# Chunked-scan stage of an encoder layer: decay prepared two chunks earlier and masked one chunk earlier, a second buffer for transposed outputs, the last group's steps over three gate blocks

## Chip, cores and metric

The kernel runs on one core of one Trainium2 chip. The metric is the device time of one launch in microseconds (us). Three runs of the kernel before took 2399.12, 2401.84 and 2405.68 us; the median is 2401.84 us. The profile is one more execution of the same program.

## What is computed

One encoder layer on 1024 tokens of width 1024, in fp32. Two token mixers read the same normed input: windowed attention with a learned sink (16 query heads, 4 key heads), and a Mamba-2 scan in both directions (32 heads in 8 groups, chunks of 128 tokens, state 128). Their outputs are projected, weighted by sigmoid gates and merged; then follow a cross-attention to 256 memory rows, a squared-ReLU MLP and a last norm. The change lies in the scan, cut here to what matters:

```
    CB = jnp.einsum('bclgn,bcsgn->bcgls', Cc, Bc)
    Wd = CB[:, :, :, None] * segsum_exp(adt)
    y_diag = jnp.einsum('bcgrls,bcsgrp->bclgrp', Wd, xdt)
    ...
    y_off = jnp.einsum('bclgn,bcgrpn,bcgrl->bclgrp', Cc, prev, jnp.exp(a_cs))
    return (y_diag + y_off).reshape(b, l, H, P)
```

`segsum_exp` is a 128x128 triangle of decays, one per head and chunk, with one triangle for each direction. `CB` is the same for the four heads of a group. After the scan, y is multiplied by silu(z) and normed within its group.

## The kernel before, in words

Every weight product on TensorE (PE) is done as three fp32r matmuls, high times high, high times low and low times high (`mm3`, the lines L85, L89 and L90); a weight tile comes by DMA and is split by ScalarE (ACT, `whi`, L66) and GpSimd (POOL, `wlo`, L69). One such product of a 128-wide weight block with all tokens has 48 matmuls, and the generator `fm_chunks` gives control back after every three, so a block has 16 units.

The scan stage (`ssd_phase`) is a list of such blocks, the jobs. For each group g there are four convolution blocks (x in two halves, then B, then C; `conv_job`), one gate block (`gate_job`) and the z block of 64 smaller units (`z_job`). While the weight products of group g run, the eight scan steps of group g-1 (chunks 7 down to 0) are slipped in: the dictionary beside each job says after which unit which piece is issued, so steps stand eight units apart. PE's order in this stage is this written order. The other engines' orders are set by a scheduler that may lift an instruction ahead of others where its inputs and buffers allow.

A step is `step(q, c)`, lines 519 to 553. It first calls `prep(q, c - 1)` for the next chunk: two DMAs from ACT's queue bring the rows of cumulated decay (`rows`, L503), POOL masks each triangle (L504, L506), ACT takes eight exponentials (`ef`, `eb`, L514 and L515), VectorE (DVE) adds the two directions (L516), PE makes `cb` = C·B (L509) and DVE multiplies `ef` by it (L517). `ef` has two buffers. Then the step itself: four matmuls of the masked decay with x (L529, into the free half of `cb`), one with the carried states (`yo`, L533), DVE scales that by the decay (`t`, L537, one buffer), POOL adds the skip term to the backward half (`p1`, L541 and L543), DVE adds the parts and multiplies by silu(z) (`yz`, L545 to L547), and ACT squares for the norm (L548). After four steps `rstd_of` (L122 on DVE, L124 on POOL) gives the norm, ACT scales the four `yz` tiles (L552), and `yt` transposes them on PE (L560); ACT copies the result to `yts` (L562, one buffer), which a DMA of SyncE's queue writes out. `cb`, `yo`, `yt`, `tm`, `st` and `zp` share one pool of PSUM slots: `yo` of a step goes into the slot that `t` of the step before has read, and the second half of `tm_b` (the transposed B, L456) into the slot of the first `yt`.

The last group has no following group to hide in. Its eight steps stand in gate blocks 8 and 9, four units apart. Gate blocks 10 to 14 belong to the attention stage that follows (`ATT_GATES`, L30), where a scheduler sets PE's order too: 10 beside key head 0, 11 beside 1, 12 beside 2, 13 and 14 beside 3.

Of the kernel before, what the change touches and what calls it, by code (L numbers as in the profile page):

```python
# [7 lines left out]
F32 = mybir.dt.float32  # L8
# [8 lines left out]
P = 128  # L17
# [9 lines left out]
SLOPES = [2.0 ** (-0.5 * (h + 1)) for h in range(16)]  # L27


ATT_GATES = ((10,), (11,), (12,), (13, 14))  # L30
END_GATE = 15


# [40 lines left out]
def wload(kx, src, n=1024, hi=None, lo=None, eng=None, pin=False):  # L74
    if hi is None:
        hi = kx.wp.tile([P, 1024], F32R, tag="wop", bufs=6, name="whi")[:, :n]
        lo = kx.wp.tile([P, 1024], F32R, tag="wop", bufs=6, name="wlo")[:, :n]
    split_in(kx, src, hi, lo, eng, pin)
    return hi, lo
# [39 lines left out]
def rstd_of(kx, pool, ss, n, width, eps):  # L119
    nc = kx.nc  # L120
    v = pool.tile([P, 8], F32, tag="rv", bufs=4, name="rv")
    nc.vector.tensor_scalar(v[:, :n], ss, 1.0 / width, eps, ALU.mult, ALU.add)  # L122
    r = pool.tile([P, 8], F32, tag="rr", bufs=4, name="rr")
    nc.gpsimd.tensor_tensor(r[:, :n], v[:, :n], kx.mhalf[:, :n], ALU.pow)  # L124
    return r
# [203 lines left out]

class Group:  # L330
    def __init__(self, g):
        self.g, self.hs, self.cx = g, slice(4 * g, 4 * g + 4), []


def fm_chunks(kx, ps, w, halves=(0, 1)):
    ws = wsplit(w)
    for h in halves:
        for k in range(NK):
            mm3(kx, ps[:, h * 512:(h + 1) * 512], ws[k], act_pair(kx.hT[h], k), k == 0, k == NK - 1)
            yield  # L340


def psum_g(kx, name):
    return kx.pg.tile([P, S], F32, tag="g", name=name)
# [46 lines left out]
def ssd_phase(kx, ins, dr):  # L391
# [3 lines left out]
    V, A, G, PE = nc.vector, nc.scalar, nc.gpsimd, nc.tensor  # L395
    with tc.tile_pool(name="p1", bufs=1) as sp, tc.manual_schedule(engines={mybir.EngineType.PE}):
# [4 lines left out]
        def heads(ap):  # L401
            return ap.rearrange("p (h q) -> p h q", h=4)
# [13 lines left out]
        def gate_job(m):  # L416
            def load():
                return wload(kx, ins["wg"][m])

            def run(w):  # L420
                ps = psum_g(kx, "gps")
                yield from fm_chunks(kx, ps, w)
                gt = ca.tile([P, 2, 512], F32, tag="tab", bufs=2, name="gt")
                for h in range(2):
                    A.activation(gt[:, h], ps[:, h * 512:(h + 1) * 512], AF.Tanh, scale=0.5)
                    nc.sync.dma_start(dr.gt[m][h], gt[:, h])
            return load, run
# [68 lines left out]

        def prep(q, c):
            b, j = c // 4, c % 4
            cl = slice(c * P, (c + 1) * P)
            rows = sp.tile([P, 2, 4, P], F32, tag="rows", bufs=2, name="rows")  # L500
            for d in range(2):
                o = 64 * d + 32 * b + 4 * q.g
                nc.scalar.dma_start(rows[:, d], dr.cs[o:o + 4, j * P:(j + 1) * P].partition_broadcast(P))  # L503
            G.affine_select(out=rows[:, 0], in_=rows[:, 0], compare_op=ALU.is_ge, fill=NEG, base=0,  # L504
                            pattern=[[0, 4], [1, P]], channel_multiplier=-1)
            G.affine_select(out=rows[:, 1], in_=rows[:, 1], compare_op=ALU.is_ge, fill=NEG, base=0,  # L506
                            pattern=[[0, 4], [-1, P]], channel_multiplier=1)
            q.cb = cb = kx.pp.tile([P, 512], F32, tag="p", name="cb")
            PE.matmul(cb[:, :P], q.BT[:, cl], q.CT[:, cl], start=True, stop=True)  # L509
            q.ef = ef = sp.tile([P, 4, P], F32, tag="ef", bufs=2, name="ef")  # L510
            eb = sp.tile([P, 4, P], F32, tag="eb", bufs=2, name="eb")
            for h in range(4):
                o = 4 * q.g + h
                A.activation(ef[:, h], rows[:, 0, h], AF.Exp, bias=kx.ebias[:, b, j, 0, o:o + 1])  # L514
                A.activation(eb[:, h], rows[:, 1, h], AF.Exp, bias=kx.ebias[:, b, j, 1, o:o + 1])  # L515
            V.tensor_tensor(ef, ef, eb, ALU.add)  # L516
            V.tensor_tensor(ef, ef, cb[:, :P].unsqueeze(1).broadcast_to([P, 4, P]), ALU.mult)  # L517

        def step(q, c):

            b, j = c // 4, c % 4
            cl = slice(c * P, (c + 1) * P)
            cb, ef = q.cb, q.ef
            if c:
                prep(q, c - 1)
            if j == 3:
                q.yz, q.ss = [None] * 4, sp.tile([P, 4], F32, tag="ss", bufs=2, name="ss")
            for h in range(4):
                PE.matmul(cb[:, 256 + 64 * h:256 + 64 * h + 64], ef[:, h], q.xtok[:, c, 64 * h:64 * h + 64],  # L529
                          start=True, stop=True)  # L530
            lo, hi = (256 if c == 0 else 0), (256 if c == NT - 1 else 512)
            yo = kx.pp.tile([P, 512], F32, tag="p", name="yo")
            PE.matmul(yo[:, lo:hi], q.CT[:, cl], q.prev[:, c].rearrange("p d q -> p (d q)")[:, lo:hi],  # L533
                      start=True, stop=True)
            d0, d1 = lo // 256, hi // 256
            t = sp.tile([P, 2, 256], F32, tag="t", bufs=1, name="t")
            V.tensor_tensor(t[:, d0:d1].rearrange("p d (h q) -> p d h q", h=4),  # L537
                            yo[:, lo:hi].rearrange("p (d h q) -> p d h q", h=4, q=64),
                            kx.ecs[:, b, j, d0:d1, q.hs].unsqueeze(3).broadcast_to([P, d1 - d0, 4, 64]), ALU.mult)
            p1 = sp.tile([P, 256], F32, tag="p1", bufs=2, name="p1")  # L540
            G.tensor_tensor(heads(p1), heads(q.xtok[:, c]), dsk[:, q.hs].unsqueeze(2).broadcast_to([P, 4, 64]), ALU.mult)  # L541
            if d1 - d0 == 2:
                G.tensor_tensor(p1, p1, t[:, 1], ALU.add)  # L543
            y = q.yz[j] = sp.tile([P, 256], F32, tag="yz", bufs=8, name="yz")
            V.tensor_tensor(y, cb[:, 256:], t[:, d0], ALU.add)  # L545
            V.tensor_tensor(y, y, p1, ALU.add)
            V.tensor_tensor(y, y, q.zs[:, c], ALU.mult)  # L547
            A.activation(q.zs[:, c], y, AF.Square, accum_out=q.ss[:, j:j + 1])  # L548
            if j == 0:
                r = rstd_of(kx, sp, q.ss, 4, 256, 4 * EPS)  # L550
                for i in range(4):
                    A.activation(q.yz[i], q.yz[i], AF.Copy, scale=r[:, i:i + 1])  # L552
                q.done = b, q.yz

        def yt(q):
            b, yz = q.done
            for f in range(2):
                pt = kx.pp.tile([P, 512], F32, tag="p", name="yt")
                for j in range(4):
                    PE.transpose(pt[:, j * P:(j + 1) * P], yz[j][:, f * P:(f + 1) * P], kx.ident)  # L560
                yo_s = sp.tile([P, 512], F32, tag="yts", bufs=1, name="yts")
                A.activation(yo_s, pt, AF.Copy, scale=kx.g_ssd[:, 2 * q.g + f:2 * q.g + f + 1])  # L562
                nc.sync.dma_start(dr.y[2 * q.g + f][:, b * 512:(b + 1) * 512], yo_s)

# [2 lines left out]
        def job(lr, at):  # L567
            jobs.append((lr, at))

        for g in range(NG):  # L570
            q, o = gs[g], gs[g - 1]
            scan = lambda *cs: [(step, o, c) for c in cs] if g else []
            if g == 0:
                job(conv_job(q, 3), {8: [(tm_x, q)]})
            else:
                job(conv_job(q, 0), {8: [(step, o, 7)], 16: [(step, o, 6)]})
                job(conv_job(q, 1), {8: [(step, o, 5)], 16: [(step, o, 4)]})
                job(gate_job(g), {8: [(step, o, 3)], 16: [(step, o, 2)]})
                job(conv_job(q, 2), {8: [(step, o, 1)], 16: [(yt, o), (step, o, 0)]})
                job(conv_job(q, 3), {8: [(tm_x, q)], 16: [(yt, o)]})  # L580
            at = {8 * c + 8: [(state, q, c)] for c in range(NT)}
            at[2] = [(tm_b, q)]
            at[64] += [(back, q), (prep, q, 7)]
            job(z_job(q), at)
        q = gs[7]
        job(gate_job(8), {4: [(step, q, 7)], 8: [(step, q, 6)], 12: [(step, q, 5)], 16: [(step, q, 4)]})
        job(gate_job(9), {4: [(step, q, 3)], 8: [(step, q, 2)], 12: [(step, q, 1)], 16: [(yt, q), (step, q, 0)]})
        w = jobs[0][0][0]()
        for n, ((_, run), at) in enumerate(jobs):
            nxt = jobs[n + 1][0][0]() if n + 1 < len(jobs) else None  # L590
# [9 lines left out]
def attn_phase(kx, ins, dr):  # L600
    nc, tc = kx.nc, kx.tc
    V, A, G, PE = nc.vector, nc.scalar, nc.gpsimd, nc.tensor
    with tc.tile_pool(name="p2", bufs=1) as ap, tc.tile_pool(name="p2r", bufs=1, side="right") as aq:
# [31 lines left out]
        for kv in range(4):  # L635
# [91 lines left out]
            for qb in range(NT):  # L727
                if qb + 2 < NT:
                    t4s[qb + 2] = scores(qb + 2)
                values(qb, t4s[qb])  # L730
            for m in ATT_GATES[kv]:
                gate_block(kx, ins, dr, m)
# [945 lines left out]
```

## Time and profile before

| what | value |
|---|---|
| median of three runs | 2401.84 us |
| the profiled execution's own time | 2404.12 us |
| its span, first to last instruction | 2402.3 us |
| granted TensorE clock, mean | 0.995 |
| PE busy | 2328.3 us, 97% |
| DVE, ACT, POOL busy | 67%, 47%, 37% |
| DMA packets' share of the span | q1 26.0%, q10 5.7% |
| scan stage with groups inside one another | about 155 to 906 us |
| last group's steps | about 906 to 949 us |
| attention stage | about 949 to 1300 us |

Times in the trace are microseconds from the span's start. A row of the timeline gives start, duration, engine, line, operation and tiles, and in square brackets how long the engine stood idle before it and who released it. A matmul's duration includes its latency, so the work of one is read from the distance of two starts. "ACTq" is ACT's instruction queue, on which a DMA is issued. A row of the waits gives who waited for whom, then the total, the number of times and the longest. A row of the windows gives the stretch and its length, the busy time of each engine with the number of its instructions, the granted clock, the DMA share and GB/s.

### The profile page before, as it was taken

The numbers are of one execution on the slowest core, as the hardware profiler recorded it, in microseconds if no ns is written. First come the engines' busy times: TensorE is split into PE (matmuls) and PEld (weight loads), VectorE is DVE, ScalarE is ACT, GpSimd is POOL, SyncE is SP. The second block draws the span as 40 slices with busy tenths as digits, with TensorE's granted clock in tenths as the row PEclk, the third lists the DMA queues.
The fourth block names the chain that finished last, engine by engine and source line by source line (L and its number), as shares of the span: only waits on it lengthen the run. The fifth ranks groups of instructions, "written<-read, shape, count | busy, mean of one in ns | idle before, by whom it ended". The sixth has DMA issues, their size and how long they took to land.

```text
span 2402.3 us, 32309 instructions
## 1 busy us (share of the span) xinstructions
PE 2328.3 (97%) x11868; PEld 1933.5 (80%) x11868; DVE 1605.9 (67%) x2528; ACT 1134.5 (47%) x2406; POOL 891.9 (37%) x833
## 2 busy tenths in 40 slices
PE   7999999999999998999999999999999999999998
PEld 6887887878788887877777888888987887788887
DVE  6757566565757665356567987975686456689984
ACT  5446354453636454378666543245553333233441
POOL 5245435263534535255442013305485444200010
PEclk9999999999999999999999999999999999999999
DMA  6324232231423222111116347302253345721301
GB/s 225 95 59 128 58 101 88 71 118 58 123 62 114 71 88 90 51 45 50 41 41 221 123 132 254 115 1 88 88 173 122 113 133 161 277 118 71 132 27 71
DMA packets 150318, 252.06 MB, mean 105 GB/s; under 512 B 11280, under 2 KB 86160, under 8 KB 150160
## 3 DMA queue, kind: packets, MB, share of 16 engines
q1 hardware_dynamic: 79264, 211.19, 26.0%
q10 hardware_dynamic: 70896, 38.81, 5.7%
q8 instruction: 94, 1.54, 0.3%
q14 instruction: 64, 0.52, 0.1%
HBM read 202.51 MB, written 47.45 MB: 104 GB/s over the span
## 4 chain that ended last, share of the span: by engine, by line
PE 54%; DVE 17%; POOL 8%; ACT 8%; issue 8%; DMA 4%; ACTq 0%; SPq 0%; POOLq 0%; DVEq 0%
PE dps L1448 10%; PE mps L1448 8%; PE pb L1243 6%; PE pc L1243 3%; PE zp L89 2%; PE zp L85 2%; PE zp L90 2%; PE st L480 2%; DVE cx L360 2%; POOL prev L495 2%; POOL wlo L69 2%; DMA rows<-d_cs 1%; POOL cb_t L494 1%; ACT whi L66 1%; PE dps L85 1%
## 5 line engine op out<-in xcount | busy, mean ns | idle before, releaser
L69 POOL TENSOR_TENSOR wlo<-raw,whi 128x1024 fp32r<-128x1024 f32 x110 | 271.0, 2465 | 625.9 <-ACT whi L66 596.9
L1448 PE MATMUL mps<-kt 128*128 128x512 f32 x1008 | 230.3, 390 | 1.2 <-DVE kt L1400 1.2
L1399 ACT ACTIVATE kt<-row 128x512 fp32r<-128x512 f32 x264 | 144.0, 619 | 184.5 <-PE dps L1448 83.0
L1448 PE MATMUL dps<-kt 128*128 128x512 f32 x1008 | 228.6, 389 | 0.0
L1448 PEld LDWEIGHTS mps<-kt 128*128 128x128 f32 x1008 | 188.8, 188 | 41.5 <-DVE kt L1400 2.5
L1448 PEld LDWEIGHTS dps<-kt 128*128 128x128 f32 x1008 | 189.2, 188 | 39.3
L85 PE MATMUL cps<-kt,whi 128*128 128x512 f32 x512 | 216.6, 423 | 0.0
L66 ACT ACTIVATE whi<-raw 128x1024 fp32r<-128x1024 f32 x112 | 118.0, 1055 | 192.7 <-DMA raw<-in_wa_dram 47.0
L90 PE MATMUL cps<-kt,wlo 128*128 128x512 f32 x512 | 200.5, 392 | 0.0
L89 PE MATMUL cps<-kt,whi 128*128 128x512 f32 x512 | 200.0, 391 | 0.0
L1400 DVE TENSOR_TENSOR kt<-row,kt 128x512 fp32r<-128x512 f32 x264 | 172.0, 699 | 3.8 <-ACT kt L1399 3.7
L124 POOL TENSOR_TENSOR rr<-rv,mhalf 128x1 f32<-128x1 f32 (+1 forms) x50 | 38.5, 771 | 215.5 <-DVE rv L122 210.1
L1189 POOL TENSOR_TENSOR wop<-w,wop 128x512 fp32r<-128x512 f32 x64 | 86.2, 1350 | 87.0 <-ACT wop L1188 78.3
L89 PEld LDWEIGHTS cps<-kt,whi 128*128 128x128 f32 x512 | 96.8, 189 | 26.0 <-issue 7.3
L85 PEld LDWEIGHTS cps<-kt,whi 128*128 128x128 f32 x512 | 96.8, 189 | 25.7 <-issue 7.2
L90 PEld LDWEIGHTS cps<-kt,wlo 128*128 128x128 f32 x512 | 96.5, 188 | 20.9
L514 ACT ACTIVATE ef<-rows,ebias 128x128 f32<-128x128 f32 x256 | 83.5, 391 | 50.2 <-PE cb L529 49.5
L85 PE MATMUL gps<-kt,whi 128*128 128x512 f32 x240 | 102.4, 427 | 0.0
L515 ACT ACTIVATE eb<-rows,ebias 128x128 f32<-128x128 f32 x256 | 84.7, 392 | 37.1 <-POOL rows L506 35.6
L685 DVE CUSTOM_DVE_ANT_0 t<-sps,bias 128x384 f32<-128x384 f32 (+1 forms) x128 | 64.2, 521 | 56.1 <-PE sps L684 55.1
L696 POOL TENSOR_SCALAR t<-t,den 128x384 f32<-128x384 f32 (+1 forms) x128 | 69.1, 559 | 83.8 <-DVE den L694 71.4
L1243 PE MATMUL pb<-kt,wop 128*128 128x512 f32 x384 | 94.7, 396 | 2.5 <-ACT c L1297 2.5
(374 smaller groups left out, 6431.3 us busy)
## 6 DMA issues: line engine op xcount, KB each, us to landing
rows<-d_cs ACTq DMA_DIRECT2D x128, 256.0 KB, 3.8
raw<-in_wssd_dram SPq DMA_DIRECT2D x48, 512.0 KB, 3.7
raw<-in_wup_dram SPq DMA_DIRECT2D x40, 512.0 KB, 3.8
d_u<-c SPq DMA_DIRECT2D x64, 256.0 KB, 2.5
row<-in_wdn_dram SPq DMA_DIRECT2D x28, 512.0 KB, 6.4
row<-d_u SPq DMA_DIRECT2D x28, 512.0 KB, 6.6
x<-in_x_dram SPq DMA_DIRECT2D x16, 512.0 KB, 5.6
raw<-in_wg_dram SPq DMA_DIRECT2D x16, 512.0 KB, 4.1
```

The source lines that it names most:

```text
L66: steps = [nc.scalar.activation(hi, raw, AF.Copy)]
L69: steps.append((eng or nc.gpsimd).tensor_tensor(lo, raw, hi.bitcast(F32), ALU.subtract))
L85: i = mm(out, l[0], r[0], start=first, stop=False)
L89: mm(out, l[0], r[1], start=False, stop=False)
L90: mm(out, l[1], r[0], start=False, stop=last)
L514: A.activation(ef[:, h], rows[:, 0, h], AF.Exp, bias=kx.ebias[:, b, j, 0, o:o + 1])
L515: A.activation(eb[:, h], rows[:, 1, h], AF.Exp, bias=kx.ebias[:, b, j, 1, o:o + 1])
L1189: self.kx.nc.gpsimd.tensor_tensor(t[:, 1], src, t[:, 0].bitcast(F32), ALU.subtract)
L1243: self.kx.nc.tensor.matmul(ps, w[:, i, ks], act[:, k, j], start=start and k == 0 and m == 0, stop=k == 3 and m == 2, skip_group_check=True)
L1399: nc.scalar.activation(t[:, j, 0], src, AF.Copy)
L1400: nc.vector.tensor_tensor(t[:, j, 1], src, t[:, j, 0].bitcast(F32), ALU.subtract)
L1448: self.kx.nc.tensor.matmul(ps[t], lt[:, k, x, ts], rt[:, k, y], start=n in (1, 2, 5) and k == 0 and m == 0, stop=k == 3 and m == 2, skip_g ...
```

## The change

Four edits. `prep` is cut in two: the DMAs, triangle masks, exponentials and their sum stay in `prep`, now called for chunk c-2 (two preps ahead of the first step, in the z block at units 56 and 64), with three `ef` buffers; the `cb` matmul and the multiply by it become `mask`, called for chunk c-1. `yts` has two buffers. The last group's steps are spread over gate blocks 8, 9 and 10, six units apart. Gate block 10 leaves the attention stage for that.

```diff
-ATT_GATES = ((10,), (11,), (12,), (13, 14))
+ATT_GATES = ((), (11,), (12,), (13, 14))
...
         def prep(q, c):
...
-            q.cb = cb = kx.pp.tile([P, 512], F32, tag="p", name="cb")
-            PE.matmul(cb[:, :P], q.BT[:, cl], q.CT[:, cl], start=True, stop=True)
-            q.ef = ef = sp.tile([P, 4, P], F32, tag="ef", bufs=2, name="ef")
+            ef = q.efs[c] = sp.tile([P, 4, P], F32, tag="ef", bufs=3, name="ef")
...
             V.tensor_tensor(ef, ef, eb, ALU.add)
+
+        def mask(q, c):
+            cl = slice(c * P, (c + 1) * P)
+            q.cb = cb = kx.pp.tile([P, 512], F32, tag="p", name="cb")
+            PE.matmul(cb[:, :P], q.BT[:, cl], q.CT[:, cl], start=True, stop=True)
+            ef = q.efs[c]
             V.tensor_tensor(ef, ef, cb[:, :P].unsqueeze(1).broadcast_to([P, 4, P]), ALU.mult)
...
-            cb, ef = q.cb, q.ef
+            cb, ef = q.cb, q.efs[c]
             if c:
-                prep(q, c - 1)
+                mask(q, c - 1)
+            if c > 1:
+                prep(q, c - 2)
...
-                yo_s = sp.tile([P, 512], F32, tag="yts", bufs=1, name="yts")
+                yo_s = sp.tile([P, 512], F32, tag="yts", bufs=2, name="yts")
...
-            at[64] += [(back, q), (prep, q, 7)]
+            at[56] += [(prep, q, 7)]
+            at[64] += [(prep, q, 6), (back, q), (mask, q, 7)]
...
-        job(gate_job(8), {4: [(step, q, 7)], 8: [(step, q, 6)], 12: [(step, q, 5)], 16: [(step, q, 4)]})
-        job(gate_job(9), {4: [(step, q, 3)], 8: [(step, q, 2)], 12: [(step, q, 1)], 16: [(yt, q), (step, q, 0)]})
+        job(gate_job(8), {6: [(step, q, 7)], 12: [(step, q, 6)]})
+        job(gate_job(9), {2: [(step, q, 5)], 8: [(step, q, 4)], 14: [(step, q, 3)]})
+        job(gate_job(10), {4: [(step, q, 2)], 10: [(step, q, 1)], 16: [(yt, q), (step, q, 0)]})
```

PE's written order inside the groups stays as it is. What the scheduler makes of the other engines is shown at two places. The first is DVE around step 2 of a group, in the middle of the stage (`ef_5852` is the decay of chunk 2, `t_5871` belongs to step 3, `yz_5788` to step 4, `rv` is the norm after step 4, `cx` the next group's convolution). Before:

```order
L547 TENSOR_TENSOR yz_5788<-yz_5788,zs_5206 128x256
L516 TENSOR_TENSOR ef_5852<-ef_5852,eb_5853 128x512
L537 TENSOR_TENSOR t_5871<-yo_5869,ecs_178 128x512
L363 SCALAR_TENSOR_TENSOR cx_5801<-th_5807,cx_5801 128x1024
L122 TENSOR_SCALAR rv_5793<-ss_5572 128x4
L517 TENSOR_TENSOR ef_5852<-ef_5852,cb_5850 128x512
L545 TENSOR_TENSOR yz_5876<-cb_5763,t_5871 128x256
```

The same place of the changed kernel, where `ef_5786` is the decay of chunk 2, `ef_5873` that of chunk 1 and `t_5891` belongs to step 3:

```order
L552 TENSOR_TENSOR yz_5808<-yz_5808,zs_5206 128x256
L520 TENSOR_TENSOR ef_5786<-ef_5786,cb_5861 128x512
L513 TENSOR_TENSOR ef_5873<-ef_5873,eb_5874 128x512
L363 SCALAR_TENSOR_TENSOR cx_5821<-th_5827,cx_5821 128x1024
L122 TENSOR_SCALAR rv_5813<-ss_5592 128x4
L542 TENSOR_TENSOR t_5891<-yo_5889,ecs_178 128x512
L513 TENSOR_TENSOR ef_5937<-ef_5937,eb_5938 128x512
L550 TENSOR_TENSOR yz_5896<-cb_5774,t_5891 128x256
```

The multiply of chunk 2 has moved from the sixth place to the second, and the `t` of step 3 from the third to the sixth.

The second place is ACT where a group ends: `xtok` and `btok` are copies of the next group's transposed x and B, `th` its convolution's tanh, `eb` an exponential of a later prep, `yts` the two halves of the second transposed output. Before (the row DMAs of that `eb` stand ahead of this piece):

```order
L457 ACTIVATE xtok_6128<-tm_6129 128x4x128
L362 ACTIVATE th_6088<-cB_6082 128x1024
L457 ACTIVATE xtok_6128<-tm_6135 128x4x128
L457 ACTIVATE xtok_6128<-tm_6141 128x4x128
L457 ACTIVATE xtok_6128<-tm_6147 128x4x128
L515 ACTIVATE eb_6705<-rows_6693,ebias_177 128x128 x4
L66 ACTIVATE whi_6520<-raw_6522 128x1024
L562 ACTIVATE yts_6182<-yt_6177,cols_212 128x512
L354 ACTIVATE cC_6193<-cps_6103,cols_212 128x1024
```

In the changed kernel:

```order
L457 ACTIVATE xtok_6128<-tm_6141 128x4x128
L362 ACTIVATE th_6088<-cB_6082 128x1024
L457 ACTIVATE xtok_6128<-tm_6147 128x4x128
L502 DMA rows_6716<-d_cs_72 128x4x128
L512 ACTIVATE eb_6726<-rows_6716,ebias_177 128x128 x2
L66 ACTIVATE whi_6540<-raw_6542 128x1024
L567 ACTIVATE yts_6182<-yt_6177,cols_212 128x512
L567 ACTIVATE yts_6190<-yt_6185,cols_212 128x512
L354 ACTIVATE cC_6193<-cps_6103,cols_212 128x1024
```

The second of the two row DMAs now stands right ahead of the exponential that reads it, behind `th`, and the two `yts` copies stand together.

More of the change, by code (lines that the diff above doesn't have):

```diff
@@ L331, in __init__ @@
     def __init__(self, g):
-        self.g, self.hs, self.cx = g, slice(4 * g, 4 * g + 4), []
+        self.g, self.hs, self.cx, self.efs = g, slice(4 * g, 4 * g + 4), [], {}
 def fm_chunks(kx, ps, w, halves=(0, 1)):
@@ L498, in prep @@
             b, j = c // 4, c % 4
-            cl = slice(c * P, (c + 1) * P)
             rows = sp.tile([P, 2, 4, P], F32, tag="rows", bufs=2, name="rows")
```

## The prediction, as put on record

> **What bounds the kernel now.** I read the page first, then PE's waits by stage, then the timelines of the engines that PE waits for.
>
> ```profile
> span 2402.3 us, 32309 instructions
> PE 2328.3 (97%) x11868; PEld 1933.5 (80%) x11868; DVE 1605.9 (67%) x2528; ACT 1134.5 (47%) x2406; POOL 891.9 (37%) x833
> ```
>
> PE is the bound: 2402.3 - 2328.3 = 74.0 us of idle time is all that any reordering can win, beside clock. The change adds and removes no work on PE, so the question is which idle stretches go. PE's waits from 155 to 860 us (the groups), then from 860 to 970 us (the last group):
>
> ```profile
> PE cb L529 <- DVE ef L517: 13.6, 14, 1.7
> PE tm L456 <- ACT yts L562: 5.6, 5, 1.7
> ...
> PE cb L529 <- DVE ef L517: 2.9, 2, 2.3
> PE yt L560 <- DVE t L537: 2.8, 1, 2.8
> PE yt L560 <- ACT yz L552: 1.7, 1, 1.7
> PE cb L529 <- DVE rv L122: 0.5, 1, 0.5
> ```
>
> So the change can reach 13.6 + 5.6 + 2.9 + 2.8 + 1.7 + 0.5 = 27.1 us of waits. Some clock hangs on them. These three windows hold waits of the list (the last column but two is the granted clock):
>
> ```profile
> 410.00:420.00 10.00, 8.28 (x34) 6.07 (x33) 8.31 (x15) 8.08 (x22) 5.45 (x6) 0.83 0.42 144
> 838.00:848.00 10.00, 8.28 (x33) 6.11 (x32) 7.66 (x14) 7.20 (x21) 5.83 (x6) 0.83 0.40 120
> 940.00:955.00 15.00, 11.23 (x48) 8.61 (x46) 10.28 (x13) 5.88 (x15) 8.01 (x7) 0.89 0.26 90
> ```
>
> In the first two stands one wait of some 1.7 us for L517, in the third those of 2.8 and others. A stretch at 0.83 over 10 us lacks 0.17 x 10 = 1.7 us of PE work, one at 0.89 over 15 us 1.65 us, together 5.0 us. The Trainium skill (TensorE: Matmul & The Clock Gate, What's actually happening) says that the array drops to half clock after at least one idle window of about 3.4 us. By that rule no wait here, the longest 2.8 us, would cost clock, and the clock terms below would be nought (a sum smaller by 3.1 us); the three rows disagree, and I go by them.
>
> **The step-2 wait of each group.** Step 2 of the group in the middle of the stage, on PE and on DVE:
>
> ```profile
> 627.87 1.08 PE L529 MATMUL cb<-xtok,ef 128*128 128x64 f32 x8 [1.72 <-DVE ef L517]
> 628.79 1.08 PE L533 MATMUL yo<-prev,cC 128*128 128x512 f32 x2
> ...
> 623.68 1.12 DVE L516 TENSOR_TENSOR ef<-ef,eb 128x512 f32<-128x512 f32 x1
> 624.72 0.68 DVE L537 TENSOR_TENSOR t<-yo,ecs 128x512 f32<-128x512 f32 x1
> 625.32 1.21 DVE L363 SCALAR_TENSOR_TENSOR cx<-th,cx 128x1024 f32<-128x1024 f32 x1
> 626.45 0.68 DVE L122 TENSOR_SCALAR rv<-ss 128x4 f32<-128x4 f32 x1
> 627.05 0.68 DVE L517 TENSOR_TENSOR ef<-ef,cb 128x512 f32<-128x512 f32 x1
> 627.65 0.41 DVE L545 TENSOR_TENSOR yz<-cb,t 128x256 f32<-128x256 f32 x1
> ```
>
> PE had been free at 627.87 - 1.72 = 626.15. Between 623.68 and 627.65 DVE ran five instructions without a gap: the sum of a prep, `t` of step 3, a convolution's end, the norm's `rv`, and last the multiply that PE wanted. DVE is the limiter for these 4 us. In the new order the multiply is first of the five, so the step's first matmul (now L534) starts at 626.15. But `t` of step 3 is now the last of the five, and PE's `yo` of step 2 goes into the PSUM slot which that `t` reads. The five are the same kinds of instruction, so `t` ends where the multiply ended, and `yo` starts at about 627.87, where L529 started before. It would have started 628.79 - 627.87 = 0.92 us after L529, at 627.07, so a wait of 0.8 us is left under a new name. What is won is 628.79 - 627.87 = 0.92 us. There are seven such places: 7 x 0.92 = 6.4 us of gain.
>
> Of the 14 waits the other seven are short ones at step 4, such as this:
>
> ```profile
> 611.04 1.07 PE L529 MATMUL cb<-xtok,ef 128*128 128x64 f32 x8 [0.30 <-DVE ef L517]
> ```
>
> There the multiply moves ahead of two DVE instructions (L516 and L363) as well, and `t` of step 5 takes its place; `yo` comes 0.92 us after L529, so `t` has cover of 0.92 - 0.30 = 0.6 us. 7 x 0.3 = 2.1 us go. Bounds for both kinds together: nothing won (if the new wait is as long as the old), and all 13.6. The clock: two of the windows above follow such waits, 3.4 us. A wait cut from 1.7 to 0.8 us may or may not still cost clock, and I take half, 1.7.
>
> **The second `yts` buffer.** Before, PE waits for the first of the two `yts` copies (the PSUM slot), and ACT comes to it late:
>
> ```profile
> 652.04 1.27 DVE L360 SCALAR_TENSOR_TENSOR cB<-cps,cols,cB 128x1022 f32<-128x1022 f32 x1
> 653.04 1.71 ACT L552 ACTIVATE yz<-yz,rr 128x256 f32<-128x256 f32 x4 [2.24 <-POOL rr L124]
> 657.51 1.27 ACT L515 ACTIVATE eb<-rows,ebias 128x128 f32<-128x128 f32 x4
> 658.68 1.05 ACT L66 ACTIVATE whi<-raw 128x1024 fp32r<-128x1024 f32 x1
> 659.63 0.68 ACT L562 ACTIVATE yts<-yt,cols 128x512 f32<-128x512 f32 x1
> 660.36 0.66 PE L456 MATMUL tm<-ident,cB 128*128 128x128 f32 x4 [0.68 <-ACT yts L562]
> ```
>
> The buffer itself frees the second copy, which PE doesn't wait for. What counts is what stands ahead of the first: now a DMA issue behind `th`, then its landing, one triangle mask, two exponentials, `whi`. How an issue behind other ACT work leaves, and how long it takes to land, the trace shows:
>
> ```profile
> 641.29 0.40 ACT L515 ACTIVATE eb<-rows,ebias 128x128 f32<-128x128 f32 x1 [1.25 <-POOL rows L506]
> 641.35 0.37 ACTq L503 DMA_DIRECT2D rows<-d_cs  x1
> 641.60 0.39 ACT L515 ACTIVATE eb<-rows,ebias 128x128 f32<-128x128 f32 x1
> 654.59 0.64 POOL L506 TENSOR_SCALAR_AFFINE_SELECT rows<-rows 128x512 f32<-128x512 f32 x1 [0.98 <-DMA rows<-d_cs]
> DMA to landing us min/median/max: 3.1/3.9/6.3
> ```
>
> The issue at 641.35 stands behind all four `eb` in ACT's order, and left when the first had only started: ACT's queue runs ahead of its arithmetic up to the next unmet wait. For the new issue that wait is `th`'s, for the last convolution step on DVE, which ends at 652.04 + 1.27 = 653.3. Landing 3.9 later, 657.2; mask 0.64, 657.85; two exponentials 0.6, `whi` 0.95, so `yts` starts at 659.4 against 659.63. That is 0.2 us earlier, 7 x 0.2 = 1.4 us of gain. With a landing of 3.1 ACT itself is the limit (eb from 657.5, `yts` at 659.05, gain 7 x 0.6 = 4.2); with 6.3 it is 2.2 us later, a loss of 15. The range takes both; the median row decides.
>
> **The last group.** PE's waits there:
>
> ```profile
> 918.32 1.08 PE L529 MATMUL cb<-xtok,ef 128*128 128x64 f32 x8 [2.27 <-DVE ef L517]
> ...
> 923.11 1.00 PE L529 MATMUL cb<-xtok,ef 128*128 128x64 f32 x8
> ...
> 927.83 1.00 PE L529 MATMUL cb<-xtok,ef 128*128 128x64 f32 x8
> ...
> 933.18 1.08 PE L529 MATMUL cb<-xtok,ef 128*128 128x64 f32 x8 [0.47 <-DVE rv L122]
> 938.81 1.08 PE L529 MATMUL cb<-xtok,ef 128*128 128x64 f32 x8 [0.65 <-DVE ef L517]
> 946.77 0.66 PE L560 MATMUL yt<-ident,yz 128*128 128x128 f32 x4 [2.79 <-DVE t L537]
> 955.67 0.33 PE L560 MATMUL yt<-ident,yz 128*128 128x128 f32 x1 [1.65 <-ACT yz L552]
> ```
>
> Steps four units apart recur every 927.83 - 923.11 = 4.72 us without a wait. In the groups two steps and sixteen units took 627.87 - 611.04 - 1.72 = 15.1 us; two steps and eight units are 2 x 4.72 = 9.4, so eight units are 5.7 us and one is 0.71. Six units apart, steps recur every 4.72 + 1.4 = 6.1 us. Step 5 now asks for its decay six units, 4.2 us, later than before, where 2.27 were missing. The steps behind it ask 1.4 us later each, and their decay's exponentials and sum are a step older. The chain that released them took 4.72 + 0.47 and 4.72 + 0.65 us, under 6.1; only the one to `yt` took 4.72 + 2.79 = 7.5, and in it stood exponentials and sum that are now a step ahead (1.2 and 0.6 us by the rows at 657.51 and 627.05, and the landing of their rows). I let all four go: 6.2 us. The wait at 955.67 is for the norm at the very end; the filler between the last step and `yt` is the same, but ACT has less behind it, so I leave 0.4 of 1.65: 1.25 gained. Together 7.4 us, and with them most of the clock stretch at 947 (1.4 of 1.65). Bounds: 5 us, if one wait of 2.8 stays, and 7.9 with the clock in full.
>
> **Attention.** Gate block 10, 11 us of PE work, is no longer there to fill waits beside key head 0. It only moves, so its own time costs nothing; what it covered may show. Two windows of that stage, the one after key head 0 begins and the last:
>
> ```profile
> 1050.00:1130.00 80.00, 79.00 (x397) 61.26 (x397) 49.94 (x143) 58.20 (x146) 40.83 (x53) 1.00 0.17 50
> 1210.00:1300.00 90.00, 87.00 (x426) 67.38 (x425) 53.17 (x142) 59.91 (x141) 36.69 (x47) 1.00 0.35 113
> ```
>
> PE idles 1.0 us where filler is plenty, 3.0 at the end. In the first, 80 - 11 = 69 us would still exceed ACT's 58.2 and DVE's 49.9. I take a loss of 1.0 us, bounds 0 and 3.
>
> **The sum.** -6.4 - 2.1 - 1.7 - 1.4 - 7.4 - 1.4 + 1.0 = -19.4 us. The profiled execution took 2404.12 us, 2.28 more than the median of the runs, 2401.84; from the one the sum gives 2384.7, from the other 2382.4. I forecast 2382.
>
> **Rivals.** (a) *All waits go.* If DVE, with its new order, runs `t` soon enough, the whole 27.1 us and 5.0 us of clock leave: 2401.84 - 32.1 = 2370. For it: nothing but order limits DVE, which is 67% busy. Against: the five instructions stand in line.
>
> (b) *The wait only changes its name.* `yo` waits for `t` as long as L529 did for the multiply, because DVE's sum (its sum took 1.12 us above, the multiply of the same size 0.68) stretches further, or `yts` eats the gain. Then only the last group counts, 7.4 + 1.4 = 8.8: 2393.
>
> (c) *Attention asks for its filler.* Key head 0 has only the next head's q products beside it. If half of the 11 us show as waits, -19.4 + 5.5 - 1.0 gives 2387; if all, 2392. Against: 79.00 of 80 busy.
>
> (d) *Slower: the row DMA stands in ACT's line.* If the issue leaves only when ACT has worked off what is ahead, it goes at 657.5 (where `eb` started); landing 661.4, mask 662.0, `yts` at 663.6, 4.0 us later than before, at seven places: 28 us. Against the sum without its 1.4: 2401.84 - 18.0 + 28 = 2412. It is slower than before by over 7.2 us once the delay exceeds (18.0 + 7.2) / 7 = 3.6 us a group. Against it stands the issue at 641.35, which ran ahead of three activations; here nine stand between. The Trainium skill (TensorE: Matmul & The Clock Gate, Architectural detail) gives ScalarE a queue of eight, strictly first in, first out. By that rule the issue could run ahead by eight at most, which leaves it nearly at 653.3 and speaks against this case; no row here shows the depth.
>
> **How the numbers follow.** Chances: forecast 0.55, (a) 0.15, (b) 0.15, (c) 0.10, (d) 0.05. 0.3% of 2401.84 is 7.2 us, about what a measurement can tell from no change. Faster by more than that: the forecast, (a), most of (b) at 2393 and of (c), 0.85. Within it: the rest of (b) and (c) and the forecast with landings near 6.3, 0.10. Slower: (d), 0.05. The range 2369 to 2397 holds the forecast's own (2401.84 less 32 to less 5: waits and clock in full; or `yts` later by 1.9 us a group, which takes 13 of 18.0), (a), (c) and all but the tail of (b); it leaves out (d).
>
> **What would show it.** In the changed trace: a row "PE yo L538 <- DVE t" of some 0.8 us at seven places and none for the multiply inside the groups; `tm` waits of 3 to 6 us in total; no wait over 1 us from 906 to 955; the last step ending 11 - 7.4 = 3.6 us later than at 949, and attention 11 us shorter. The forecast is wrong if the `yo` wait is near 1.7 or near nought, if `yts` starts after 661, or if PE waits for `sps` or `pt` early in the attention.

## The result

Four runs of the changed kernel took 2383.61 to 2387.91 us, median 2385.33; the kernel before, on the same chip, 2403.02. The ratio is 0.9929, 95% interval 0.9914 to 0.9943: 17.7 us faster, where 19.4 were forecast. The profiled execution took 2387.91 us. Its page:

```profile
span 2386.1 us, 32289 instructions
PE 2321.6 (97%) x11868; PEld 1931.8 (81%) x11868; DVE 1575.5 (66%) x2528; ACT 1137.3 (48%) x2406; POOL 890.7 (37%) x833
```

PE's idle time fell from 74.0 to 2386.1 - 2321.6 = 64.5 us, by 9.5; PE's busy time fell by 6.7 us with the same instructions, which can be clock and shorter first matmuls behind waits. PE's waits in the groups (155 to 860 us), then around the last group (840 to 985):

```profile
PE tm L456 <- ACT yts L567: 11.8, 6, 2.0
PE tm L456 <- DVE cB L363: 0.6, 1, 0.6
...
PE yt L565 <- ACT yz L557: 2.0, 1, 2.0
PE tm L456 <- ACT yts L567: 1.8, 1, 1.8
PE cb L534 <- DVE ef L520: 1.3, 1, 1.3
```

All 14 waits for the masked multiply, 13.6 us, are gone, and nothing stands in their place: there is no row of `yo` waiting for `t`. But `tm` waits for `yts` at every one of the seven group ends, six in the first window and one at 864 us in the second, 11.8 + 1.8 = 13.6 us, where it was 5.6; a wait of 0.6 for the B convolution comes on top. In the last group 2.0 + 1.3 = 3.3 us are left of 7.9. So -13.6 + 8.0 + 0.6 - 4.6 = -9.6, about the change in idle time. The forecast had 16.3 us of waits (6.4 + 2.1 + 1.4 + 7.4 - 1.0) and 3.1 us of clock; what came is 9.5 us of idle time and 6.7 of busy time. The total lies near the forecast because its terms were off both ways, and that is luck. Three of the signs that the prediction named speak against its working: the `yo` wait is near nought, the `tm` waits are 13.6 us instead of 3 to 6, and two waits over 1 us are left in the last group.

**Why `yo` didn't wait.** The same place as in the prediction, DVE and then PE:

```profile
616.43 0.68 DVE L520 TENSOR_TENSOR ef<-ef,cb 128x512 f32<-128x512 f32 x1
617.03 1.09 DVE L513 TENSOR_TENSOR ef<-ef,eb 128x512 f32<-128x512 f32 x1
618.04 1.65 DVE L363 SCALAR_TENSOR_TENSOR cx<-th,cx 128x1024 f32<-128x1024 f32 x1
619.61 0.16 DVE L122 TENSOR_SCALAR rv<-ss 128x4 f32<-128x4 f32 x1
619.68 0.68 DVE L542 TENSOR_TENSOR t<-yo,ecs 128x512 f32<-128x512 f32 x1
...
619.56 0.38 PE L518 MATMUL cb<-cC,cB 128*128 128x128 f32 x2
...
620.62 1.08 PE L538 MATMUL yo<-prev,cC 128*128 128x512 f32 x2
```

The five stand in the order that the prediction read, and take about as long: 619.68 + 0.6 - 616.43 = 3.85 us against 3.97. But they begin 619.56 - 616.43 = 3.1 us ahead of PE's `cb`, where it had been 625.78 - 623.68 = 2.1 (the `cb` row of before is below). `t` ends at about 620.3, and `yo` starts at 620.62 unhindered, with some 0.1 us to spare beyond the 0.2 that a release took in the prediction's rows (DVE done with the multiply at 627.65, L529 at 627.87). Where the 1.0 us came from shows in the add of step 4 and POOL's weight split beside it, measured from the first matmul of step 3, in the kernel before:

```profile
618.55 1.00 PE L529 MATMUL cb<-xtok,ef 128*128 128x64 f32 x8
...
625.78 0.38 PE L509 MATMUL cb<-cC,cB 128*128 128x128 f32 x2
...
619.75 2.45 DVE L546 TENSOR_TENSOR yz<-yz,p 128x256 f32<-128x256 f32 x1
...
619.53 2.39 POOL L69 TENSOR_TENSOR wlo<-raw,whi 128x1024 fp32r<-128x1024 f32 x1 [1.57 <-ACT whi L66]
```

and in the changed kernel:

```profile
612.34 1.00 PE L534 MATMUL cb<-xtok,ef 128*128 128x64 f32 x8
...
613.53 0.42 DVE L551 TENSOR_TENSOR yz<-yz,p 128x256 f32<-128x256 f32 x1
...
615.05 1.46 DVE L552 TENSOR_TENSOR yz<-yz,zs 128x256 f32<-128x256 f32 x1
...
613.71 2.51 POOL L69 TENSOR_TENSOR wlo<-raw,whi 128x1024 fp32r<-128x1024 f32 x1 [1.64 <-ACT whi L66]
```

An add of two SBUF tiles takes 0.42 us alone; begun 0.2 us after POOL's split it ran until about the split's end, 2.45 us. DVE comes to the add 1.2 us behind step 3's first matmul both times (619.75 - 618.55 and 613.53 - 612.34). What moved is the split: it starts 1.4 us behind that matmul instead of 1.0, so the add is now 0.2 us ahead of it. A convolution instruction with an operand in PSUM follows and takes 1.28 us, as it does without the split; then the multiply of two SBUF tiles is held, for 1.46. From the add to the first of the five DVE takes 616.43 - 613.53 = 2.9 us, where it took 623.68 - 619.75 = 3.9, and this is the whole 1.0 us. The kernel before shows the same on its own: in its first two groups the split came 1.8 and 1.9 us behind the matmul, the add took 0.41 and 0.42 us, and the waits at step 2 were 1.43 and 1.52 us instead of 1.7. Why the split starts later in the changed kernel was not followed. The Trainium skill (Trainium Architecture — The Big Picture, What this means for kernel authors) says that VectorE and GpSimd share a port pair under an exclusive lock. The trace agrees: 2.45 against 0.42 us.

**Why `tm` waits longer.** The chain from step 2 of a group to its end, across POOL, DVE, ACT and PE of the changed kernel:

```profile
625.31 2.37 POOL L69 TENSOR_TENSOR wlo<-raw,whi 128x1024 fp32r<-128x1024 f32 x1 [0.27 <-ACT whi L66]
627.64 0.73 POOL L548 TENSOR_TENSOR p<-p,t 128x256 f32<-128x256 f32 x1
...
628.40 0.43 DVE L551 TENSOR_TENSOR yz<-yz,p 128x256 f32<-128x256 f32 x1 [4.26 <-POOL p L548]
...
630.22 0.42 ACT L553 ACTIVATE zs<-yz 128x256 f32<-128x256 f32 x1 [3.82 <-DVE yz L552]
630.22 0.37 ACTq L502 DMA_DIRECT2D rows<-d_cs  x1
...
634.43 0.64 POOL L505 TENSOR_SCALAR_AFFINE_SELECT rows<-rows 128x512 f32<-128x512 f32 x1 [3.16 <-DMA rows<-d_cs]
...
645.60 1.28 DVE L360 SCALAR_TENSOR_TENSOR cB<-cps,cols,cB 128x1022 f32<-128x1022 f32 x1
...
650.24 1.18 POOL L505 TENSOR_SCALAR_AFFINE_SELECT rows<-rows 128x512 f32<-128x512 f32 x1 [2.76 <-DMA rows<-d_cs]
...
653.00 1.24 ACT L567 ACTIVATE yts<-yt,cols 128x512 f32<-128x512 f32 x2
...
653.72 0.66 PE L456 MATMUL tm<-ident,cB 128*128 128x128 f32 x4 [2.03 <-ACT yts L567]
```

POOL now does the weight split ahead of its add to `p`; in the kernel before the add came first:

```profile
632.30 0.74 POOL L543 TENSOR_TENSOR p<-p,t 128x256 f32<-128x256 f32 x1
633.83 2.38 POOL L69 TENSOR_TENSOR wlo<-raw,whi 128x1024 fp32r<-128x1024 f32 x1 [0.80 <-ACT whi L66]
```

DVE waits 4.26 us for that add. ACT's square waits for DVE, and the row DMA of a prep that was lifted in from the next group is issued behind that square. Its landing, its mask and its exponentials then stand ahead of everything else that ACT has to do for the group's end. The convolution of B ends at 645.60 + 1.28 = 646.88, the last row DMA leaves then, and its landing, its mask, two exponentials and a weight split stand ahead of `yts`. PE's own steps don't see any of it until `tm`, 25 us later.

But this chain did not grow. In the kernel before the split held DVE's multiply instead, for 2.54 us, and ACT's square came at 636.52, 18.0 us behind step 3's first matmul (618.55); now it comes 630.22 - 612.34 = 17.9 behind. The convolution of B ended 653.31 - 618.55 = 34.8 us behind that matmul, and now ends 34.5 behind. From there to `yts` it took 6.3 us, and now takes 6.1. It is PE that comes sooner: it was ready for `tm` at 660.36 - 0.68 = 659.68, 41.1 us behind the matmul, and now at 653.72 - 2.03 = 651.69, 39.4 behind, because its wait of 1.72 us at step 2 is gone. It is 1.8 us sooner and `yts` 0.4, so `tm` waits 1.4 us longer, 2.03 instead of 0.68. The seven groups are alike: PE is ready 40.9 to 42.2 us behind the matmul before and 39.2 to 40.0 now, and the convolution ends 34.8 to 35.8 and 34.1 to 35.2 behind. Most of the wait that PE lost at step 2 it meets again at `tm`.

### The profile page after: what moved, and what is told of

It reads as the page before. It is cut to its first block, busy times and chain, and to the rows that moved or that the text cites. A ratio compares the mean times of both kernels' runs of the same rounds, so it can differ in the third digit from the quotient of the medians.

```text
span 2386.1 us, 32289 instructions
## 1 busy us (share of the span) xinstructions
PE 2321.6 (97%) x11868; PEld 1931.8 (81%) x11868; DVE 1575.5 (66%) x2528; ACT 1137.3 (48%) x2406; POOL 890.7 (37%) x833
## 4 chain that ended last, share of the span: by engine, by line
PE 56%; DVE 16%; POOL 8%; ACT 8%; issue 6%; DMA 5%; ACTq 0%; SPq 0%; POOLq 0%; DVEq 0%
PE dps L1455 10%; PE mps L1455 8%; PE pb L1250 6%; PE pc L1250 3%; PE zp L89 2%; PE zp L85 2%; PE zp L90 2%; PE st L480 2%; POOL wlo L69 2%; DMA rows<-d_cs 2%; ACT whi L66 2%; POOL prev L495 1%; DVE cx L360 1%; PE dps L89 1%; PE dps L85 1%
```

## The experiments

The first theory was that the second `yts` buffer did the harm, since it goes with the row DMA behind `th`. The rival was the earlier prep. All ratios are to the kernel before on the same chip, with 95% intervals.

**yts_only.** The kernel before, with

```diff
-                yo_s = sp.tile([P, 512], F32, tag="yts", bufs=1, name="yts")
+                yo_s = sp.tile([P, 512], F32, tag="yts", bufs=2, name="yts")
```

> The kernel before with the second yts buffer alone. Theory: this edit lets the scheduler put both copies together and push the second row DMA behind the tanh, so the exponentials that read it, the weight split and the first copy come late; PE's waits of tm for yts go from 5.6 us to 13 or more in total, the waits for the multiply stay near 13.6, and the kernel is some 8 us slower than before. Rival (the prep two chunks ahead is what fills ACT there): tm waits at or below 5.6 us, the time within 2 us of before.

2404.66 us, ratio 1.0003 (0.9994 to 1.0013): no difference. PE's waits from 155 to 1000 us:

```profile
PE cb L529 <- DVE ef L517: 16.1, 14, 2.3
PE tm L456 <- ACT yts L562: 6.0, 6, 1.8
```

In the kernel before these are 16.6 and 5.6 us over the same stretch. The theory falls. ACT's order is the one that the front part shows for the changed kernel, DMA behind `th`, and `tm` still waits only 6.0 us.

**after_yts1.** The changed kernel with that edit undone:

```diff
-                yo_s = sp.tile([P, 512], F32, tag="yts", bufs=2, name="yts")
+                yo_s = sp.tile([P, 512], F32, tag="yts", bufs=1, name="yts")
```

> The changed kernel with one yts buffer again. Theory: tm waits fall from 13.6 us in total to about 6, the step waits stay at nought, the time is some 8 us below the changed kernel, near 0.990 of before. Rival: tm waits stay above 12 us, the time equals the changed kernel's, 0.993.

2388.34 us, ratio 0.9946 (0.9935 to 0.9958). `tm` waits 12.3 us. The theory fails here as well. The median is 3 us above the changed kernel's, but the intervals overlap; five short waits of `yt` for an `xtok` copy (2.1 us) are new.

**prep_only.** The kernel before with `prep` and `mask` as in the changed kernel, `ATT_GATES`, the last group's jobs and `yts` as before. Against the changed kernel:

```diff
-ATT_GATES = ((), (11,), (12,), (13, 14))
+ATT_GATES = ((10,), (11,), (12,), (13, 14))
...
-                yo_s = sp.tile([P, 512], F32, tag="yts", bufs=2, name="yts")
+                yo_s = sp.tile([P, 512], F32, tag="yts", bufs=1, name="yts")
...
-        job(gate_job(8), {6: [(step, q, 7)], 12: [(step, q, 6)]})
-        job(gate_job(9), {2: [(step, q, 5)], 8: [(step, q, 4)], 14: [(step, q, 3)]})
-        job(gate_job(10), {4: [(step, q, 2)], 10: [(step, q, 1)], 16: [(yt, q), (step, q, 0)]})
+        job(gate_job(8), {4: [(step, q, 7)], 8: [(step, q, 6)], 12: [(step, q, 5)], 16: [(step, q, 4)]})
+        job(gate_job(9), {4: [(step, q, 3)], 8: [(step, q, 2)], 12: [(step, q, 1)], 16: [(yt, q), (step, q, 0)]})
```

> The kernel before with the prep two chunks ahead and the early multiply alone; yts has one buffer and the last group's steps stand in two gate blocks. Theory: all 13.6 us of step waits in the groups go and one or two half-clock windows with them, tm waits stay near 6, the last group keeps most of its 7.9 us; 14 to 17 us below before, about 0.9935. Rival: tm waits grow to 12 or more and 7 to 9 us are left of the gain, about 0.997.

2391.96 us, ratio 0.9960 (0.9947 to 0.9973). PE's wait for `yts` from 155 to 1000 us:

```profile
PE tm L456 <- ACT yts L567: 12.3, 7, 1.8
```

The rival holds in the waits: the prep edit takes the 13.6 us of step waits in the groups and, by itself, makes `tm` wait 12.3 us. The time, 11.4 us below before, lies between the two.

**rows3.** The changed kernel with

```diff
-            rows = sp.tile([P, 2, 4, P], F32, tag="rows", bufs=2, name="rows")
+            rows = sp.tile([P, 2, 4, P], F32, tag="rows", bufs=3, name="rows")
```

> The changed kernel with three row buffers, so that a row DMA needs not wait for the exponentials of the prep before. Theory (the landing of a row DMA stands ahead of yts): tm waits fall below 6 us, time some 8 us below the changed kernel, 0.990 of before. Rival (two copies together and a later convolution copy make it late, not the DMA): tm waits stay at 12 to 14 us, time as the changed kernel.

2407.74 us, ratio 1.0018 (1.0009 to 1.0027). Neither theory foresaw that it loses all the gain. PE's waits from 155 to 1000 us:

```profile
PE tm L456 <- DVE cB L363: 12.1, 7, 1.9
PE yo L538 <- DVE t L542: 6.1, 11, 0.8
PE tm L456 <- ACT yts L567: 5.1, 7, 0.8
```

The chain is longer here: the convolution of B ends 37.0 to 39.1 us behind step 3's first matmul instead of 34.1 to 35.2, and `tm` waits for it. That the scheduler, with another buffer, lifts still more of the next preps ahead is the likely reason, but it was not shown. And here are the waits of `yo` for `t` that the prediction named, 0.4 to 0.8 us at step 2 of all seven groups; the other four, of 0.2 to 0.4 us, are at step 3.

The second theory followed the chain above: DVE's wait for POOL's add at step 2. Its test lets DVE do that add.

**dve2.** The changed kernel with

```diff
-            if d1 - d0 == 2:
+            if d1 - d0 == 2 and c not in (2,):
                 G.tensor_tensor(p1, p1, t[:, 1], ALU.add)
...
             V.tensor_tensor(y, cb[:, 256:], t[:, d0], ALU.add)
+            if d1 - d0 == 2 and c in (2,):
+                V.tensor_tensor(y, y, t[:, 1], ALU.add)
```

> The changed kernel, but in step 2 DVE itself adds the backward half of t (one more 128x256 add there), so that DVE need not wait for POOL's add behind the weight split wlo. Theory: this wait of 4.3 us on DVE makes ACT's square, the row DMA issued behind it, the mask, the exponentials and at last yts late; without it the tm waits fall from 13.6 us in total to 6 or less and the time by 6 to 10 us, to about 0.990 of before. Rival (the row DMAs' own chain of buffers and landings holds ACT, whatever POOL does): tm waits stay at 12 to 14 us, the time within 2 us of the changed kernel, 0.993.

2375.74 us, ratio 0.9886 (0.9872 to 0.9901), 26 us below before and 9.6 below the changed kernel. DVE's timeline at step 2, and PE's waits from 155 to 860 us:

```profile
618.52 0.42 DVE L552 TENSOR_TENSOR yz<-yz,t 128x256 f32<-128x256 f32 x1
618.98 0.74 DVE L553 TENSOR_TENSOR yz<-yz,p 128x256 f32<-128x256 f32 x1
...
PE tm L456 <- ACT yts L569: 7.2, 7, 1.9
```

The wait of 4.26 us is gone, `tm` waits fall from 13.6 to 7.2, and no wait for the multiply is left. The last group's 1.3 us are not this edit's doing: they hung on the add of step 3, which POOL still does (see below). The theory holds in the main; 7.2 is above the 6 that it named. The convolution of B now ends 32.8 to 34.3 us behind step 3's first matmul, and the `yts` copies still begin 6.1 us behind its end. The two longest `tm` waits, 1.85 and 1.93 us, are in the groups where it ends latest, at 34.2 and 34.3. What holds it there is open.

**dve21.** The same for steps 2 and 1:

```diff
-            if d1 - d0 == 2 and c not in (2,):
+            if d1 - d0 == 2 and c not in (1, 2):
...
-            if d1 - d0 == 2 and c in (2,):
+            if d1 - d0 == 2 and c in (1, 2):
```

> As dve2, for steps 2 and 1. Theory: the wait of DVE for POOL at step 1 (1.55 us, behind a mask that waits for a row DMA) goes too, tm waits fall below 5 us in total, 1 to 3 us less than dve2. Rival: as dve2, no change against the changed kernel.

2375.88 us, ratio 0.9886 (0.9870 to 0.9901), `tm` waits 7.9 us: the same as dve2. Taking away DVE's wait at step 1 wins nothing.

**gates_only.** The kernel before with two places of the change:

```diff
-ATT_GATES = ((10,), (11,), (12,), (13, 14))
+ATT_GATES = ((), (11,), (12,), (13, 14))
...
-        job(gate_job(8), {4: [(step, q, 7)], 8: [(step, q, 6)], 12: [(step, q, 5)], 16: [(step, q, 4)]})
-        job(gate_job(9), {4: [(step, q, 3)], 8: [(step, q, 2)], 12: [(step, q, 1)], 16: [(yt, q), (step, q, 0)]})
+        job(gate_job(8), {6: [(step, q, 7)], 12: [(step, q, 6)]})
+        job(gate_job(9), {2: [(step, q, 5)], 8: [(step, q, 4)], 14: [(step, q, 3)]})
+        job(gate_job(10), {4: [(step, q, 2)], 10: [(step, q, 1)], 16: [(yt, q), (step, q, 0)]})
```

> The kernel before with the last group's steps over three gate blocks and gate block 10 out of the attention, nothing else. Theory: the waits from 906 us on go from 7.9 to about 3 us, step waits and tm waits in the groups stay at 13.6 and 5.6, attention gives back 1 to 2 us; 4 to 6 us below before, 0.998. Rival (attention needs that filler): PE waits for pt, op or sps grow by 5 us or more, the time equal to before or above.

2398.18 us, ratio 0.9984 (0.9975 to 0.9993): a small gain, 4 us. PE's waits from 155 to 1000 us:

```profile
PE cb L529 <- DVE ef L517: 12.7, 14, 1.7
PE tm L456 <- ACT yts L562: 5.7, 5, 1.7
PE yt L560 <- ACT yz L552: 2.7, 1, 2.7
```

Of the last group's 7.9 us only the final 2.7 is left. In the attention `op` waits 1.4 us for `pl`, at most 0.8 at a time, where it was 0.3; the rival falls.

**dve_extra.** The changed kernel with a line behind the masked multiply:

```diff
             V.tensor_tensor(ef, ef, cb[:, :P].unsqueeze(1).broadcast_to([P, 4, P]), ALU.mult)
+            V.tensor_tensor(ef, ef, ef, ALU.max)
```

> The changed kernel with one more DVE instruction of 0.6 us (a maximum of the decay with itself) behind each masked multiply. Theory (yo of step 2 starts 0.1 us after the slot is free, so DVE's five instructions are as near the path as forecast): PE waits of yo for t appear, some 0.5 us at seven steps 2 and 0.2 at seven steps 4, 4 to 6 us in total, the time 5 to 9 us above the changed kernel. Rival (t has ample cover): no such waits, the time within 2 us of it.

2420.51 us, ratio 1.0073 (1.0057 to 1.0089), 35 us above the changed kernel. PE's waits from 155 to 1000 us:

```profile
PE cb L535 <- DVE ef L521: 13.7, 12, 2.0
...
PE yo L539 <- DVE t L543: 4.6, 7, 0.7
```

Waits of `yo` came, 4.6 us at seven places, but all of them at step 4, 0.66 us each. At step 2 there is none; there the scheduler put the maximum behind the convolution's end, so the decay itself is late, and in three groups PE waits 1.6 to 2.0 us for that. So this run shows how near the path `t` is at step 4 in its own order, and for step 2 only rows3 shows it. The size was missed: the old waits are back.

**dve2_yts1.** dve2 with one `yts` buffer:

```diff
-                yo_s = sp.tile([P, 512], F32, tag="yts", bufs=2, name="yts")
+                yo_s = sp.tile([P, 512], F32, tag="yts", bufs=1, name="yts")
```

> The kernel dve2 with one yts buffer, so that the row DMA stands ahead of the tanh again. Theory: with POOL's wait gone, what is left of the tm waits (7.2 us in dve2) is that DMA's landing, 1.6 us a group on ACT; tm waits fall to 3 us or less and the time by 3 to 6 us against dve2, to 0.987 of before. Rival (the second buffer helps by itself, as the changed kernel's 3 us below its version with one buffer may say): tm waits stay at 6 to 8 us, waits of yt for xtok appear, the time is 1 to 3 us above dve2.

2378.78 us, ratio 0.9905 (0.9888 to 0.9921). `tm` waits 8.7 us instead of 7.2. The theory falls: the landing of the last row DMA is not what is left. Whether the second buffer helps by itself stays open, as the intervals overlap; but in both pairs (this one, and after_yts1 beside the changed kernel) the kernel with one buffer has the median that is 3 us higher.

**dve2_sync.** dve2 with the row DMAs on SyncE's queue:

```diff
-                nc.scalar.dma_start(rows[:, d], dr.cs[o:o + 4, j * P:(j + 1) * P].partition_broadcast(P))
+                nc.sync.dma_start(rows[:, d], dr.cs[o:o + 4, j * P:(j + 1) * P].partition_broadcast(P))
```

> The kernel dve2 with the row DMAs issued from SyncE's queue instead of ACT's. Theory: a row DMA no longer stands behind ACT's squares and copies, ACT never waits for a mask in front of yts; tm waits fall to 3 us or less, the time 3 to 6 us below dve2. Rival: row DMAs that wait for a buffer hold the weight loads behind them on SyncE's queue, or the new order puts other waits in their place; the time is above dve2 by 3 us or more.

2430.05 us, ratio 1.0107 (1.0091 to 1.0123). PE's waits from 155 to 1000 us, then POOL, ACT and the clock at one of the long waits:

```profile
PE yt L567 <- ACT yz L559: 26.4, 8, 4.0
...
341.63 0.63 POOL L503 TENSOR_SCALAR_AFFINE_SELECT rows<-rows 128x512 f32<-128x512 f32 x1 [5.92 <-DMA rows<-d_cs]
343.90 1.71 ACT L559 ACTIVATE yz<-yz,rr 128x256 f32<-128x256 f32 x4 [3.69 <-POOL rr L124]
...
342.00:352.00 10.00, 7.54 (x37) 6.78 (x38) 1.49 (x2) 7.51 (x15) 4.24 (x4) 0.66 0.19 61
```

The rival holds: the wait moves to `yt`, 3.5 to 4.0 us a group, and the clock is down behind each. In the group shown the row DMAs leave SyncE's queue at 336.17, behind the DMA of an output and that of a weight. POOL's mask waits 5.92 us for its rows, the norm `rr` stands behind two masks in POOL's queue, ACT's scaling of `yz` waits 3.69 us for `rr`, and `yt` waits for that.

## Why the prediction was right, and where it wasn't

**Steps 2 and 4: -8.5 forecast, -13.6 measured.** That the multiply moves to the front of DVE's five held. What failed is "`t` ends where the multiply ended". It was counted from the end of step 4's last DVE instruction in the old trace, as if DVE came to it no sooner; DVE came 1.0 us sooner against PE, and the rows above put all of it down to POOL's weight split, which starts 0.4 us later, behind step 4's add. The prediction has no term for that. That `yo` after `t` is next on the path was right: rows3 brings the wait out at step 2, at up to 0.8 us. So at this place rival (a) came true, by luck and by a margin of about 0.1 us.

**The `yts` copies: -1.4 forecast, +8.6 measured.** The step read the last few instructions of ACT well, in size too: from the convolution's end to `yts` it takes 6.1 us with two buffers (the changed kernel, yts_only, dve2) and 6.3 in nearly every group with one (the kernel before, after_yts1, prep_only, dve2_yts1): the 0.2 us a group that were forecast. The issue left at 646.93 when the convolution step that `th` needs had ended, before `th` itself began:

```profile
646.93 0.37 ACTq L502 DMA_DIRECT2D rows<-d_cs  x1
...
648.35 1.06 ACT L362 ACTIVATE th<-cB 128x1024 f32<-128x1024 f32 x1
```

The queue did run ahead, and rival (d) is out. What came true in part is the end of rival (b), that `yts` eats some of the gain. What failed is "`yts` starts at 659.4 against 659.63": both are times of the old trace, as if PE came to `tm` when it did before. PE came 1.8 us sooner, because its wait at step 2 was gone, and the convolution's end only 0.2. The prediction added two gains that are not independent: with the convolution's end where it was, the 0.92 us that it gave to step 2 would have made `tm` wait 0.92 - 0.2 = 0.7 us longer in a group like this one. prep_only shows it without the second buffer: 12.3 us of `tm` waits. dve2 shows that DVE's wait for POOL's add carries nearly half of them (13.6 to 7.2). The other 7.2 are the convolution's end, still too late for PE; what holds it is not settled, and the second buffer and the last DMA are not it by yts_only and dve2_yts1.

**The last group: -7.4 forecast, -4.6 measured in waits.** Three of the five went as said. Two were missed:

```profile
929.05 1.08 PE L534 MATMUL cb<-xtok,ef 128*128 128x64 f32 x8 [1.27 <-DVE ef L520]
...
926.68 0.43 DVE L551 TENSOR_TENSOR yz<-yz,p 128x256 f32<-128x256 f32 x1 [4.28 <-POOL p L548]
...
925.30 0.64 POOL L505 TENSOR_SCALAR_AFFINE_SELECT rows<-rows 128x512 f32<-128x512 f32 x1 [4.65 <-DMA rows<-d_cs]
```

The add at 926.68 belongs to step 3. Ahead of POOL's part of it, in POOL's queue, stands a mask that waits 4.65 us for its row DMA; DVE waits behind both, and step 2's multiply behind that. The decay was a step older, as the step said, but the queue that it went through was not looked at. The wait hangs on one long landing: the mask starts 5.7 us after that DMA was issued (919.64). In after_yts1 and dve2 the same mask stands ahead of the same add and starts 3.6 and 3.9 us after the issue, and there step 2 doesn't wait. So the 1.3 us are shown for this one execution and not for an edit; why this DMA took longer is open. And the final wait for the norm, hoped at 0.4, is 2.0; it is 1.0 in after_yts1 and 2.7 in gates_only.

**Clock: -3.1 forecast, about -1.7 measured in this stage.** Two stretches below full clock are left where there were three:

```profile
436.00:446.00 10.00, 7.38 (x47) 6.76 (x45) 5.00 (x5) 7.27 (x13) 3.33 (x2) 0.83 0.37 122
945.00:960.00 15.00, 12.99 (x58) 10.44 (x57) 1.77 (x4) 6.92 (x15) 3.21 (x5) 0.89 0.36 132
```

They now follow a `tm` wait and the final wait for the norm. The rest of the 6.7 us by which PE's busy time fell (other stages, first matmuls behind waits) was not separated; over the whole span the mean granted clock is 0.997 instead of 0.995.

**Attention: +1.0 forecast.** From the first `vp` matmul to the first `mps` it takes 1273.3 - 959.1 = 314.2 us instead of 1287.9 - 964.1 = 323.8. That is 9.6 less without the gate block of 11, a loss of about 1.4. In gates_only it takes 1280.4 - 966.5 = 313.9. Rival (c) is out, as 79.00 busy of 80 had said.

The parts add up about: prep_only -11.4, gates_only -3.9, yts_only +1.3 against the 2403.33 and 2402.03 us of before beside them, -14.0 in all against -17.7. The intervals of prep_only (3 us either way) and of the changed kernel (3.5) leave room for the rest. after_yts1, which has the edits of prep_only and gates_only, is 15.0 us below its before, against 11.4 + 3.9 = 15.3: these two add up.

## What to carry to other kernels

When a wait on the bound engine goes, that engine comes sooner to all that follows. Count every chain that ends on it later anew against its new arrival: the slack that the wait gave them is gone too, and a gain here and a gain there don't simply add. An add that sits behind a long instruction in another engine's queue can be cheaper on the engine that needs it, even if that is the busier one: one more 0.42-us add on DVE gave 9.6 us. Where a scheduler sets the order, a buffer more isn't free: a third `rows` buffer cost all 18 us.

## What the runs showed of the hardware

In dve2_sync waits of 3.6 and 3.9 us on PE were followed by a granted clock of 0.66 over 10 us (230 to 240, and 342 to 352 above), 3.4 us of lost work each. In the kernel before one wait of some 1.7 us was followed by 0.83 over 10 us at 410 to 420 and at 838 to 848, 1.7 us lost each, while the waits at step 2 of the other five groups, 1.4 to 1.7 us, were not; the one at 627.87 left the clock at 1.00:

```profile
590.00:700.00 110.00, 107.31 (x601) 90.37 (x600) 68.95 (x97) 54.34 (x131) 52.83 (x56) 1.00 0.31 89
```

The Trainium skill (TensorE: Matmul & The Clock Gate, What's actually happening) asks for an idle window of about 3.4 us. The waits of dve2_sync agree with that, those of 1.7 us do not: half as much idle time is enough at some places and not at others (in two of seven groups of the kernel before; of the seven `tm` waits of 1.7 to 2.0 us in the changed kernel, one), and a wait can cost as much again as it lasts.

A third `rows` buffer and the move of one DMA to another queue, both meant to free ACT, cost 22 and 54 us against the kernels that they were made from (2407.74 against 2385.33, 2430.05 against 2375.74).
